# The opening of a two-layer block: row tiles loaded in six pieces, the filters' first layer in another PSUM bank, the second conditioning chunk straight behind the first

## The chip, the cores and the metric

The kernel runs on one core of a Trainium2 chip. A core has TensorE (PE; its weight loads are listed apart as PEld), VectorE (DVE), ScalarE (ACT), GpSimd (POOL) and SyncE (SP), which here issues all transfers of the opening. Results of TensorE go to PSUM. The metric is the device time of one execution in microseconds (us), as the median of several runs.

## The reference

Two layers act on a sequence `x` of 512 rows and a context `ctx` of 256 rows, each row 1024 wide. Every layer has conditioned norms, a mixer and a convolutional feed-forward part. Layer 0 mixes with Fourier transforms and a long convolution (hyena), layer 1 with attention. What the opening computes is this:

```python
sh1, sc1, g1, sh2, sc2, g2 = _adaln(c, w_mod[0], b_mod[0])    # silu(c) @ w_mod + b_mod, in six parts
hx = _modulate(_rms_norm(x, norm1[0]), sh1, sc1)              # rms_norm * (1 + sc1) + sh1
csh1, csc1, ... = _adaln(c_ctx[None, :], w_mod[0], b_mod[0])
hc = _modulate(_rms_norm(ctx, norm1[0]), csh1, csc1)
proj = h @ w_in                                               # first projection of the mixer, h = hx or hc
...
h = jnp.sin(f * (z @ _f32(w1) + _f32(b1)))                    # hyena filters, layer by layer
h = jnp.sin(f * (h @ _f32(w2) + _f32(b2)))
h = jnp.sin(f * (h @ _f32(w3) + _f32(b3)))
```

## The kernel before

Rows lie along the free axis and the 1024 features along partitions. So `x` is eight row tiles of 128 partitions (`KD` = 8), each 772 columns wide: 512 columns of `x`, two of zeros, 256 columns of `ctx` from column `C0` = 514 on, and two of zeros. Matmuls are split in three (`mm3`): a high part of weight and operand, made on ACT (`hi`, L133), and a low part, made on VectorE (`lo`, L138).

The opening is in `mixer`, under a manual schedule: PE, VectorE, ACT and SyncE execute in the order in which the code is written. In that order:

- SyncE loads the filters' tables (`zT`, `fw`), then `x` in eight transfers of 256 KB (L460) and `ctx` in eight of 128 KB (L462). Behind them come two conditioning chunks `wm` of 2 MB in two halves each (`gemv_raw`, L209) and three tiles of the projection's weight (`wraw`, L146). The pool of chunks has two buffers, so the third chunk's load waits for the first chunk's matmuls.
- PE computes the filters' first layer (`layer(0, None, 0)`, L410), then `spare(8)`. `spare(n)` is n matmuls of the identity with a constant tile into a PSUM bank that is overwritten later; their result is not used. In the profile each counts as two passes of L470.
- The norms: `s1(d)` and `s2(d)` square row tile d on ACT (L267), for `x` and then for `ctx`, and add it up on VectorE (L274). `f1(True, 0)` and `f2(True, 0)` fold the sums over partitions on PE (L280) and take the reciprocal root on VectorE (L167 to L176). `f1(True, 1)` and `f2(True, 1)` spread the root over partitions on PE (L298) and copy it out of PSUM on ACT (L301).
- Conditioning: `gemv_pe` multiplies a chunk on PE (L219) and copies the result on ACT (L222). The function that it returns (`g0`, `g1`: the turn) turns it into columns on PE (L227) and adds the bias on VectorE (L232). Scale and shift of the norm's first four row tiles need chunks 0 and 1.
- `layer(0, pa, 1)` is the sine's argument on VectorE (L384 to L393), step 2 the sine itself on ACT (L414).
- `both(d, 0)` makes the normalised high part of row tile d (L308 on VectorE, L309 on ACT), `both(d, 1)` the low part (L313), and `first(m, k)` is the projection of row tile k onto output tile m (L158 to L160).

PSUM is given out in two kinds: `mm`, three tiles of two banks, all three held by the projection (`ps3`), and `ms`, two tiles of one bank. Norm folds, spreads, gemvs, turns and the filters' layers take turns with the two `ms` tiles.

Of the kernel before, what the change touches and what calls it, by code (L numbers as in the profile page):

```python
# [9 lines left out]
F32 = mybir.dt.float32  # L10
# [8 lines left out]
P = 128  # L19
D = 1024  # L20
KD = 8
T = 512
C = 256
C0 = 514
TW = 772
# [60 lines left out]
class Builder:  # L86
# [309 lines left out]
    def filter_mlp(self):  # L396

        nc, I = self.nc, self.I
        p = self.pf
        zT = self.t(p, [66, 384], F32, "zT")  # L400
        fw = self.t(p, [P, 3, P], F32, "fw")
        self.w4 = self.t(p, [P, 1024], F32, "w4")
        nc.sync.dma_start(zT, I["zT"])
        nc.sync.dma_start(fw, I["fw"])

        def layer(l, h, step):
            if step == 0:
                ps = self.ms()
                K = 66 if l == 0 else P
                nc.tensor.matmul(ps[:, :384], fw[:K, l, :], (zT if l == 0 else h)[:K, :384], start=True, stop=True)  # L410
                return ps
            if step == 1:
                return self.sine(h, self.col(f"fb{l + 1}"))
            nc.scalar.activation(h[:, :384], h[:, :384], AF.Sin)  # L414
            return h

        return layer
# [15 lines left out]
    def mixer(self):  # L433
        nc, I = self.nc, self.I
        v = nc.vector
        self.S2 = self.pool("S2", bufs=19)
        xp = self.pool("xp", side="right")
# [7 lines left out]
            v.memset(self.onesN[nh], nh)  # L445
        self.altr = self.t(self.pf, [P, 1], F32R, "altr")
        v.tensor_copy(self.altr, self.alt)
        x = [self.t(xp, [P, TW], F32, f"x{d}") for d in range(KD)]
        hh, hl = [], []
        (s1, f1, a1), (s2, f2, a2) = self.norm(0, 0, x, hh, hl, 0, T, tp), self.norm(0, 0, x, hh, hl, C0, C, tp)  # L450
        self.bscale = 1.0
# [3 lines left out]
        with self.tc.manual_schedule(engines={ENG.PE, ENG.DVE, ENG.SP, ENG.Activation}):  # L455
            layer = self.filter_mlp()
            warm = tp()[:, 0:256]
            v.memset(warm, 1.0)
            for d in range(KD):
                nc.sync.dma_start(x[d][:, 0:512], I["xT"][d])  # L460
            for d in range(KD):
                nc.sync.dma_start(x[d][:, C0 : C0 + C], I["cxT"][d])  # L462
            wm = [self.gemv_raw(0), self.gemv_raw(1)]
            win = [self.wraw(I["w_in"][m]) for m in range(3)]
            ps3 = [self.mm() for _ in range(3)]

            def spare(n):

                for _ in range(n):
                    nc.tensor.matmul(ps3[2][:, 512:768], self.ident, warm, start=True, stop=True)  # L470

            pa = layer(0, None, 0)
            spare(8)
            for d in range(KD):
                s1(d)
            for d in range(KD):
                s2(d)
            f1(True, 0)
            spare(5)
            f2(True, 0)  # L480
            spare(3)
            f1(True, 1)
            g0 = self.gemv_pe(0, 0, wm[0])
            wm.append(self.gemv_raw(2))
            f2(True, 1)
            h = layer(0, layer(0, pa, 1), 2)
            g0()
            spare(3)
            wins = [self.wsplit(win[0])]
            g1 = self.gemv_pe(0, 1, wm[1])  # L490
            spare(1)
            wm.append(self.gemv_raw(3))
            nc.sync.dma_start(self.w4, I["w4"])
            for tt in (4, 5):
                dec[tt] = tp()
                nc.sync.dma_start(dec[tt], I["decay"][tt])
            wins.append(self.wsplit(win[1]))
            g1()
            self.make_A(0, 0, b=4)
            for d in range(KD):  # L500
                hh.append(self.t(hp, [P, TW], F32R, f"hh{d}"))
                hl.append(self.t(hp, [P, TW], F32R, f"hl{d}"))
            self.zero_pads(hh + hl)

            def both(d, step):
                a1(d, step)
                return a2(d, step)

            def first(m, k):
                self.proj_k(ps3[m], wins[m], hh, hl, k)

            pa = layer(1, h, 0)
            spare(5)
            both(0, 0)
            both(1, 0)
            both(0, 1)
            first(0, 0)
            first(1, 0)  # L520
            wins.append(self.wsplit(win[2]))
            both(1, 1)
            both(2, 0)
            first(0, 1)
            first(1, 1)
            both(3, 0)
            both(2, 1)
            first(2, 0)
            first(2, 1)
            g2 = self.gemv_pe(0, 2, wm[2])  # L530
            both(3, 1)
            h = layer(1, layer(1, pa, 1), 2)
            first(0, 2)
            g2()
            first(1, 2)
            first(2, 2)
            g3 = self.gemv_pe(0, 3, wm[3])
            first(0, 3)
            g3()
            self.make_A(0, 0, a=4)  # L540
            first(1, 3)
            first(2, 3)
            self.close("wm")
            self.pg = self.pool("pg")
            for d in range(4, KD + 1):
                if d < KD:
                    last_act = both(d, 0)
                if d > 4:
                    last = both(d - 1, 1)
                    for m in range(3):  # L550
                        first(m, d - 1)
                if d == 6:
                    pa = layer(2, h, 0)
                if d == 4:
                    self.filter_w4()
            h3 = layer(2, layer(2, pa, 1), 2)
            nc.sync.dma_start(self.brow, I["hyb"].partition_broadcast(P))
            for j in range(2):
                nc.sync.dma_start(self.sb[:, j, :], I["cboth"][j : j + 1, :].partition_broadcast(P))
# [1386 lines left out]
```

## Time and profile before

| | |
|---|---|
| median of 3 runs | 1623.88 us (1619.55 to 1624.58) |
| the profiled execution | 1623.17 us |
| its span, first to last instruction | 1621.4 us |
| mean granted TensorE clock | 0.993 |
| loads, mean over the span | 107 GB/s |
| loads, first 45 us | 356 GB/s |

The span is what the profile shows; the execution's own time has 1.8 us more around it. "Busy" is the union of an engine's instructions; DMA issues and waits on SyncE are not counted as busy. A row of the timeline gives start, length, engine, line, operation, output<-input and count, and in brackets the idle time of the engine before it with what ended it. The chain of waits follows back from the last instruction to whatever released each step. "DMA to landing" runs from the issue of a transfer to the arrival of its last byte's signal.

### The profile page before, as it was taken

To read this page: it belongs to the slowest core of one execution; us is meant where nothing else is said; L and a number is where in the kernel's file an instruction comes from. 1 tells how busy PE (TensorE), PEld (TensorE's weight loads), DVE (VectorE), ACT (ScalarE), POOL (GpSimd) and SP (SyncE) were. 2 spreads that over 40 slices of the span, in tenths; PEclk is the share of its full clock that TensorE was granted. 3 is DMA by queue.
4 is the path that set the end of the run, shared out by engine and by line. 5 is a ranking of instruction groups with operands and counts; after the bars stand their busy time and mean duration, and the time that the engine had idled before them with its cause. 6 is when DMAs were issued, how large, how long until landed. Compare 5 with 4: busy or idle time off the path is not lost.

```text
span 1621.4 us, 20798 instructions
## 1 busy us (share of the span) xinstructions
PE 1585.4 (98%) x8248; PEld 1295.8 (80%) x8248; DVE 1047.0 (65%) x1702; ACT 620.5 (38%) x883; POOL 108.7 (7%) x165
## 2 busy tenths in 40 slices
PE   7999998999999999999999999999999999999999
PEld 5787888888888888888888887666559878878887
DVE  6789869878786354643354586899987544344243
ACT  4441234434222212322123246998954433233131
POOL 0022134000000000000000001122210000000000
PEclk9999998999999999999999999999999999999999
DMA  9336412533443143431343210000034233233222
GB/s 355 107 116 214 163 36 76 191 118 108 166 156 130 65 143 130 156 131 65 111 140 110 91 57 20 13 11 14 0 105 142 79 104 104 78 104 104 78 91 91
DMA packets 54541, 173.35 MB, mean 107 GB/s; under 512 B 6187, under 2 KB 9453, under 8 KB 53421
## 3 DMA queue, kind: packets, MB, share of 16 engines
q1 hardware_dynamic: 54445, 172.03, 30.8%
q8 instruction: 65, 1.06, 0.3%
q14 instruction: 31, 0.25, 0.0%
HBM read 166.24 MB, written 5.77 MB: 106 GB/s over the span
## 4 chain that ended last, share of the span: by engine, by line
PE 82%; DVE 13%; ACT 2%; issue 2%; POOL 1%; DMA 1%; SPq 0%; POOLq 0%; ACTq 0%; DVEq 0%
PE mm L158 24%; PE mm L160 24%; PE mm L159 24%; PE pv L1614 2%; DVE S L1590 2%; DVE junk L243 1%; DVE wl L138 1%; PE s L1560 1%; DVE wr L1629 1%; ACT wh L133 1%; PE mm L616 1%; DVE mx L1574 0%; PE k L159 0%; PE ms L219 0%; PE k L160 0%
## 5 line engine op out<-in xcount | busy, mean ns | idle before, releaser
L158 PE MATMUL mm<-hh,wh 128*128 128x512 f32 (+2 forms) x1360 | 479.8, 355 | 1.8 <-ACT wh L133 0.9
L159 PE MATMUL mm<-hl,wh 128*128 128x512 f32 (+2 forms) x1360 | 477.9, 352 | 2.3 <-DVE hl L313 2.3
L160 PE MATMUL mm<-hh,wl 128*128 128x512 f32 (+2 forms) x1360 | 477.2, 351 | 1.6 <-DVE wl L138 1.6
L133 ACT ACTIVATE wh<-wr 128x1024 fp32r<-128x1024 f32 (+1 forms) x192 | 197.8, 1033 | 571.8 <-PE mm L159 530.4
L138 DVE TENSOR_TENSOR wl<-wr,wh 128x1024 fp32r<-128x1024 f32 (+2 forms) x192 | 230.9, 1205 | 235.8 <-ACT wh L133 229.2
L158 PEld LDWEIGHTS mm<-hh,wh 128*128 128x128 f32 x1360 | 256.2, 189 | 49.0 <-issue 7.6
L159 PEld LDWEIGHTS mm<-hl,wh 128*128 128x128 f32 x1360 | 256.4, 189 | 39.2 <-DVE hl L313 3.5
L160 PEld LDWEIGHTS mm<-hh,wl 128*128 128x128 f32 x1360 | 256.2, 188 | 37.5 <-DVE wl L138 2.2
L243 DVE SCALAR_TENSOR_TENSOR junk<-wr,sb 128x1024 bf16<-128x1024 f32 x128 | 156.1, 1219 | 41.2 <-DMA wr<-wmodT 41.1
L160 PE MATMUL mm<-ah,wl 128*128 128x512 f32 (+1 forms) x480 | 172.2, 359 | 0.0
L158 PE MATMUL mm<-ah,wh 128*128 128x512 f32 (+1 forms) x480 | 172.0, 359 | 0.0
L159 PE MATMUL mm<-al,wh 128*128 128x512 f32 (+1 forms) x480 | 171.7, 358 | 0.0
L1143 DVE SCALAR_TENSOR_TENSOR xr<-mm,mod,xr 128x512 f32<-128x512 f32 (+1 forms) x100 | 61.6, 630 | 153.8 <-PE mm L160 153.6
L159 PEld LDWEIGHTS mm<-al,wh 128*128 128x128 f32 x480 | 90.4, 188 | 14.4 <-DVE al L138 0.2
L158 PEld LDWEIGHTS mm<-ah,wh 128*128 128x128 f32 x480 | 90.3, 188 | 14.2 <-issue 0.3
L160 PEld LDWEIGHTS mm<-ah,wl 128*128 128x128 f32 x480 | 90.3, 188 | 14.1
L1614 PE MATMUL pv<-S,V 128*128 128x512 f32 x192 | 93.8, 597 | 2.5 <-ACT S L1593 2.5
L1175 ACT ACTIVATE fg<-fg 128x772 f32<-128x772 f32 (+1 forms) x44 | 32.6, 741 | 97.8 <-DVE fg L375 91.1
L1568 ACT ACTIVATE S<-s,rks 128x512 f32<-128x512 f32 x96 | 62.7, 686 | 12.4 <-PE pv L1614 8.5
L1614 PEld LDWEIGHTS pv<-S,V 128*128 128x128 f32 x192 | 34.4, 190 | 34.8 <-issue 29.4
L1590 DVE TENSOR_TENSOR S<-S,mx 128x1536 f32<-128x1536 f32 x32 | 55.3, 1749 | 2.3 <-POOL mx L1586 2.3
L1586 POOL PARTITION_ALL_REDUCE mx<-mx x16 | 44.9, 2806 | 163.2 <-DVE mx L1583 163.2
(337 smaller groups left out, 2263.1 us busy)
## 6 DMA issues: line engine op xcount, KB each, us to landing
wr<-w_up SPq DMA_DIRECT2D x88, 512.0 KB, 3.2
wr<-wmodT SPq DMA_DIRECT2D x80, 512.0 KB, 3.2
wr<-w_dn SPq DMA_DIRECT2D x32, 512.0 KB, 3.3
wm<-wmod0a SPq DMA_DIRECT2D x8, 1024.0 KB, 10.3
wr<-w_in SPq DMA_DIRECT2D x16, 512.0 KB, 4.2
wr<-w_out SPq DMA_DIRECT2D x13, 512.0 KB, 3.5
wr<-w_dn SPq DMA_DIRECT2D x17, 384.0 KB, 3.1
wr<-w_o SPq DMA_DIRECT2D x11, 512.0 KB, 3.3
```

The lines of the kernel that those rows point to most:

```text
L133: self.nc.scalar.activation(dst, src, AF.Copy)
L138: (eng or self.nc.vector).tensor_tensor(dst, src, hi.bitcast(F32), op=ALU.subtract)
L158: mmul(out, wh, xh, start=start, stop=False)
L159: mmul(out, wh, xl, start=False, stop=False)
L160: mmul(out, wl, xh, start=False, stop=stop)
L243: nc.vector.scalar_tensor_tensor(junk, raw, 1.0, self.sb[:, j, :], op0=ALU.mult, op1=ALU.mult, accum_out=acc)
L1143: nc.vector.scalar_tensor_tensor(x[m][:, a2:b2], ps[:, a2:b2], mod[:, 8 * sec + m, c : c + 1], x[m][:, a2:b2], op0=ALU.mult, op1=ALU.add)
L1175: nc.scalar.activation(g[:, :n], g[:, :n], AF.Silu)
L1568: nc.scalar.activation(c.S[a][j // 3][:, j % 3, :], c.ps[a, j], AF.Copy, scale=c.r[:, g : g + 1])
L1586: nc.gpsimd.partition_all_reduce(c.m[a][:, 1, :], c.m[a][:, 0, :], P, bass.bass_isa.ReduceOp.max)
L1590: v.tensor_tensor(c.S[a][h], c.S[a][h], mb.to_broadcast([P, 3, T]), op=ALU.subtract)
L1614: nc.tensor.matmul(c.P[a], V[:, j, o : o + 128], c.S[a][j // 3][:, j % 3, :], start=j == 0, stop=j == 5)
```

## The change

All row tiles become one tile `xx` of 128 x 8 x 772; `x[d]` is a view of it, and everything behind the opening uses these views as it used the tiles. `x` is loaded in four transfers of two row tiles, `ctx` in two transfers of four, each 512 KB. The filters' first layer writes to `ps3[1]` instead of an `ms` tile. Of the spare matmuls, five become four, three become one, and another three go. The second chunk's `gemv_pe` and the load of the fourth chunk come directly behind the first chunk's turn, ahead of the split of the first weight tile.

```diff
-        def layer(l, h, step):
+        def layer(l, h, step, ps=None):
             if step == 0:
-                ps = self.ms()
+                ps = self.ms() if ps is None else ps
...
-        x = [self.t(xp, [P, TW], F32, f"x{d}") for d in range(KD)]
+        xx = self.t(xp, [P, KD, TW], F32, "x")
+        x = [xx[:, d, :] for d in range(KD)]
...
-            for d in range(KD):
-                nc.sync.dma_start(x[d][:, 0:512], I["xT"][d])
-            for d in range(KD):
-                nc.sync.dma_start(x[d][:, C0 : C0 + C], I["cxT"][d])
+            for d in range(0, KD, 2):
+                nc.sync.dma_start(xx[:, d : d + 2, 0:512], I["xT"][d : d + 2].rearrange("d p n -> p d n"))
+            for d in range(0, KD, 4):
+                nc.sync.dma_start(xx[:, d : d + 4, C0 : C0 + C], I["cxT"][d : d + 4].rearrange("d p n -> p d n"))
...
-            pa = layer(0, None, 0)
+            pa = layer(0, None, 0, ps3[1])
             spare(8)
...
             f1(True, 0)
-            spare(5)
+            spare(4)
             f2(True, 0)
-            spare(3)
+            spare(1)
             f1(True, 1)
             g0 = self.gemv_pe(0, 0, wm[0])
             wm.append(self.gemv_raw(2))
             f2(True, 1)
             h = layer(0, layer(0, pa, 1), 2)
             g0()
-            spare(3)
+            g1 = self.gemv_pe(0, 1, wm[1])
+            wm.append(self.gemv_raw(3))
             wins = [self.wsplit(win[0])]
-            g1 = self.gemv_pe(0, 1, wm[1])
             spare(1)
-            wm.append(self.gemv_raw(3))
             nc.sync.dma_start(self.w4, I["w4"])
```

## The prediction

> **What bounds the kernel now.** I read the page first, then the chain of waits from 0 to 60 us, then the timeline of the same stretch, last the DMA view and the table by stretches. From the page:
>
> ```profile
> span 1621.4 us, 20798 instructions
> PE 1585.4 (98%) x8248; PEld 1295.8 (80%) x8248; DVE 1047.0 (65%) x1702; ACT 620.5 (38%) x883; POOL 108.7 (7%) x165
> ```
>
> TensorE is busy 98% of the span, so a change to other engines pays only where TensorE has nothing useful to do. One such place is the opening, up to the first projection matmul. The chain there (start, length, what):
>
> ```profile
> 6.28 5.77 DMA x<-xT
> ...
> 19.42 1.40 PE mm L470 x6
> 20.82 0.91 PE ms L298 x8
> 21.75 0.59 ACT s L301
> 22.39 1.97 PE ms L219 x16
> 24.38 0.60 ACT s L222
> 25.02 0.72 PE ms L298 x4
> 25.77 0.38 ACT s L301
> 26.19 1.05 PE ms L227 x8
> 27.25 1.40 PE mm L470 x6
> 28.65 1.90 PE ms L219 x16
> 30.62 0.59 ACT s L222
> 31.21 0.97 ACT wh L133
> 32.20 1.23 DVE wl L138
> ```
>
> L470 is the spare matmul, whose result nobody reads (two passes each, so x6 is spare(3)); it stands in the chain twice for 1.40 us. L219 is a conditioning chunk (gemv), L227 its turn, L298 the spread of a norm's factor, L133 and L138 the split of a weight. The timeline adds what the chain hides:
>
> ```profile
> 2.96 3.75 SPq L460 DMA_DIRECT2D x<-xT  x8
> 6.44 1.26 ACT L267 ACTIVATE s<-x 128x512 f32<-128x512 f32 x2 [1.04 <-DMA x<-xT]
> 6.76 5.64 SPq L462 DMA_DIRECT2D x<-cxT  x8
> 8.69 6.67 ACT L267 ACTIVATE s<-x 128x512 f32<-128x512 f32 x14 [0.99 <-DMA x<-xT]
> 9.35 8.18 DVE L274 TENSOR_TENSOR s<-s,s 128x512 f32<-128x512 f32 x13 [0.93 <-ACT s L267]
> 12.45 2.11 SPq L209 DMA_DIRECT2D wm<-wmod0a  x4
> ...
> 19.62 0.16 DVE L176 SCALAR_TENSOR_TENSOR rq_r<-rq_b,rq_r 128x4 f32<-128x4 f32 x1
> ...
> 21.75 0.16 DVE L176 SCALAR_TENSOR_TENSOR rq_r<-rq_b,rq_r 128x2 f32<-128x2 f32 x1 [0.52 <-PE ms L298]
> ...
> 22.42 0.67 DVE L384 TENSOR_SCALAR s<-ms,pcol 128x384 f32<-128x384 f32 x1
> ...
> 25.70 0.36 DVE L393 TENSOR_SCALAR s<-s 128x384 f32<-128x384 f32 x1
> ...
> 28.36 1.06 ACT L133 ACTIVATE wh<-wr 128x1024 fp32r<-128x1024 f32 x1 [1.68 <-DMA wr<-w_in]
> ...
> 32.91 2.32 PE L470 MATMUL mm<-s,cst 128*128 128x256 f32 x10
> 35.29 0.51 PE L158 MATMUL mm<-hh,wh 128*128 128x512 f32 x1
> ```
>
> Three things are to be seen. The sums of squares on VectorE end at 17.53 and its reciprocal root at 19.78, yet the spread starts only behind the spare matmuls. The gemv at 22.39 waits for the copy that empties a small PSUM bank: the filters' first layer has held one of the two since 5.7 us, until L384 reads it at 22.42. And the loads are a limit of their own:
>
> ```profile
> SPq L462 <- DMA x<-xT: 2.2, 6, 0.6
> ```
>
> This row of SyncE's waits says that six context transfers were held back until an earlier transfer landed. The transfers behind them, the second half of gemv chunk 1 and the second w_in, by their issue and by the time from issue to landing:
>
> ```profile
> 13.86 0.70 SPq L209 DMA_DIRECT2D wm<-wmod0a  x1
> wm<-wmod0a SPq DMA_DIRECT2D x1, 1024.0 KB, 13.2
> wr<-w_in SPq DMA_DIRECT2D x1, 512.0 KB, 13.3
> ```
>
> The half lands at 27.1. The w_in row is of the issue that follows the first w_in's, at about 16.3, and lands at 29.6; the first has landed by 28.36 by ACT's wait above. Behind 35 us TensorE hardly waits at all; its largest wait from 35 to 200 us, in total, times and longest, is
>
> ```profile
> PE mm L159 <- DVE hl L313: 2.3, 3, 0.9
> ```
>
> It waits there for VectorE's low parts, and these move along with the first projection. So what the opening gains or loses should reach the end whole.
>
> **The change, part by part.**
>
> *Loads in pieces.* Sixteen issues become six. The bytes and the runs in memory (2 KB and 1 KB) stay. A piece of two row tiles is usable only when its second half is there. From the squares' rows, tiles 2 to 7 come between 8.69 and 12.05 (the chain's last x landing), so 0.67 us apiece. The square of tile 0 therefore starts some 0.6 later than 6.44, and that of tile 2 at about 9.35 instead of 8.69. VectorE's adds run back to back from 9.35 to 17.53, so the whole row moves by about 0.65: sums end at 18.15, the first reciprocal root at 20.4. Bounds: nothing later, if fewer and larger transfers run 10% faster, and 1.3 later, if the pieces land one tile apart more. I take 0.65. [...]
>
> SyncE gets free early: four pieces and two context pieces at about 0.47 each end near 5.8 instead of 12.4, and the eight-in-flight limit then lets the wm and w_in issues follow landings, from about 6 on. What that is worth:
>
> ```profile
> 9.00:11.00 2.00, 2.00 (x7) 1.56 (x6) 1.44 (x3) 1.90 (x4) 0.00 (x0) 1.00 1.02 388
> 13.00:15.00 2.00, 0.92 (x9) 0.92 (x9) 1.69 (x5) 2.00 (x8) 0.00 (x0) 1.00 0.90 283
> 15.00:17.00 2.00, 2.00 (x7) 1.64 (x7) 1.69 (x4) 0.35 (x2) 0.00 (x0) 0.51 0.96 377
> 17.00:19.00 2.00, 2.00 (x9) 1.63 (x7) 1.65 (x10) 0.00 (x0) 0.00 (x0) 0.64 1.00 406
> 23.00:25.00 2.00, 1.31 (x16) 0.13 (x4) 1.86 (x5) 0.59 (x1) 0.00 (x0) 1.00 0.99 416
> 50.00:60.00 10.00, 9.14 (x59) 6.64 (x59) 6.02 (x14) 4.37 (x8) 0.00 (x0) 1.00 0.09 30
> ```
>
> (columns: busy time of PE, PEld, DVE, ACT, POOL; granted clock, DMA share, GB/s.) At 13 to 15 us the loads run at 283 GB/s instead of 388: 105 GB/s for 2 us is 0.21 MB, or 0.5 us at 388. That dip is the queue running dry before wm, and I count it as removed. The gemv half then lands at 26.6, the two w_in at 27.8 and 29.1. Bounds: nothing gained, and 1.5 us, if late single engines of the queue catch up too.
>
> *First layer in another bank.* No instruction is added. The bank is one that the projections first write after 33 us, and the sine reads it by 23. Both small banks are then free, so the gemv no longer waits for the copy L301 (0.59), nor the second spread for the copy L222.
>
> *Fewer spares.* The spread now follows one spare, not three. It starts with its factor at 20.4, 0.25 earlier than now despite the later sums, and ends at 21.45. Gemv 0 follows at once: 21.5 to 23.4. VectorE's second root loses its 0.52 wait but starts 0.62 later, so ends about 22.6; the second spread runs to 24.1, the copies on ACT to 24.5 (0.60 and 0.38), the turn of chunk 0 to 25.2. It now ends at 27.25: two microseconds are gone. The sine keeps its length (22.42 to 26.06 now) and starts 0.1 later.
>
> *Second chunk behind the first turn.* spare(3) (1.40) is gone from ahead of it, and the split of the first w_in stands behind its copy on ACT. What is late next is the load: the gemv could start at 25.2, but its second half of 0.95 waits for 26.6 and ends at 27.6. The reissue of the buffer, gemv_raw(3), stands behind it in SyncE's queue with w4 and the decays, all earlier by the same. On ACT: copy to 28.25, then both splits, 1.06 each, to 30.4 (both w_in are there). Today the first split lies in ACT's idle time before the copy; now it is on the path, and this gives back 1.06 of the gain. VectorE's split of the second w_in takes 1.23, to 31.65. Today it ends at 33.43 and the first projection starts 1.86 behind it; with that the first projection starts at 33.5.
>
> *Sum.* 35.29 less 33.5 is 1.8 us gained. With the load no earlier it is 1.3 (everything behind the gemv half moves by 0.5); with the load 1.5 earlier the gemv runs 25.2 to 27.1, and it is 2.3. The profiled execution took 1623.17 us, its span 1621.4 and 1.8 around it, 0.7 under the median of the runs, 1623.88. Less 1.8 that gives 1621.4. About 0.3% (4.9 us) is what a measurement of this kernel can tell from no change: the three runs alone lie 5.0 apart.
>
> **The rivals.**
>
> *The gain is swallowed behind 35 us.* Loads for the filter stage come off the same queue, and if they land no earlier, TensorE waits where it did not. Time: 1623.2. Against it: from 50 to 60 us the queue moves 30 GB/s, so the opening's loads are done by then. For it: VectorE and GpSimd work behind 42 us in an order of their own.
>
> *The granted clock drops once or twice more.* After 13 to 15 us, with TensorE busy 0.92 of 2 us, the clock was 0.51 and then 0.64: (1 − 0.51) × 2 + (1 − 0.64) × 2 = 1.7 us of TensorE's time lost. Six spares fewer leave it emptier between 23 and 33. One such drop there, where gemv, turn, layer and spare(5) stand one behind the other ahead of the first projection, takes the gain: 1623.1. Two in a row make it 1624.8, slower than before. It decides when a stretch falls to about 0.92 in 2 us. By my sum, 25.2 to 33.5 holds 1.90 (gemv) + 1.05 (turn) + 2.32 (spares) + about 1.2 (layer and one spare, at the spares' rate by columns) = 6.5 of 8.3 us, or 1.6 in 2, above the 1.31 of 23 to 25 where the clock stayed at 1.00. So it is unlikely. [...]
>
> *The pieces are waited for across columns.* In one tile the context columns of four row tiles stretch, first to last, over the others' x columns. If waits go by that extent, the squares of tiles 1 to 3 wait for a context piece, at 13.5 by the landing pace, and the sums end near 23.3, 5.1 later than in my sum; 0.4 of this is slack at the gemv's load, and the first projection comes at about 38.1: 1626.0. Against it: today's square at 6.44 did not wait for context columns of the same tile, issued from 6.76 on; but those two ranges do not interleave.
>
> *The change does not do what it says* only where the pieces would land as singles do; that is the lower bound of the 0.65.
>
> **How the numbers follow.** Forecast 0.60 (1620.9 to 1621.9 by the bounds of the load); swallowed 0.16; clock 0.08; columns 0.06; something that none of these rows shows, 0.05 to either side. The likeliest gives 1621.4. The range takes in the cases up to the clock's, and on both sides half of the 5.0 us over which the runs spread: 1618.5 to 1625.5. Faster by over 4.9 us needs more than any row here offers: 0.07. Slower by over 4.9 needs the worst case and more: 0.07. Within: 0.86.
>
> **What would show it.** Right: six issues that end by about 6 us and wm issues from then on; sums that end near 18.1; gemv 0 starting straight behind the first spread near 21.5 with no wait for L301; gemv 1 stalled in its middle by its load until about 26.6; the first projection at 33 to 34; granted clock 1.00 from 20 us on. Wrong: squares that wait past 13 us (columns), a granted clock under 1 between 24 and 35 (gate), or a new TensorE wait between 35 and 100 us (swallowed). A time outside the range with a first projection near 33.5 would say that the opening does not reach the end.

## The result, and the profile after

| | before | changed |
|---|---|---|
| median | 1621.74 us (1619.17 to 1624.58, 18 runs) | 1624.84 us (1620.99 to 1628.63, 18 runs) |
| ratio | | 1.0023, 95% interval 1.0016 to 1.0029 |
| the profiled execution | 1623.17 us | 1626.17 us |
| its mean granted clock | 0.993 | 0.990 |

The change makes the kernel slower, by some 0.2%. The page of the changed kernel shows nearly the same work (twelve TensorE passes fewer, those of the six spares) in a longer span:

```profile
span 1624.4 us, 20766 instructions
PE 1585.1 (98%) x8236; PEld 1296.0 (80%) x8236; DVE 1047.6 (64%) x1702; ACT 620.1 (38%) x883; POOL 108.6 (7%) x165
```

**The opening came out as forecast.** The timeline of the changed kernel from 2 to 36 us (start, length, engine, line; in brackets the idle time and what ended it):

```profile
2.97 2.35 SPq L461 DMA_DIRECT2D x<-xT  x4
5.37 1.91 SPq L463 DMA_DIRECT2D x<-cxT  x2
7.32 3.29 SPq L209 DMA_DIRECT2D wm<-wmod0a  x4
8.12 1.15 ACT L267 ACTIVATE s<-x 128x512 f32<-128x512 f32 x2 [2.51 <-DMA x<-xT]
10.36 8.18 DVE L274 TENSOR_TENSOR s<-s,s 128x512 f32<-128x512 f32 x13 [0.36 <-ACT s L267]
...
20.94 1.13 PE L298 MATMUL ms<-cst,rq_r 128*128 128x128 f32 x8 [0.41 <-DVE nrm_s L285]
22.00 1.92 PE L219 MATMUL ms<-wm,sT 128*32 128x512 f32 x16
23.85 0.71 PE L298 MATMUL ms<-cst,rq_r 128*128 128x128 f32 x4
24.63 1.05 PE L227 MATMUL ms<-cst,s 128*128 128x2 f32 x8
25.61 1.92 PE L219 MATMUL ms<-wm,sT 128*32 128x512 f32 x16
28.14 2.01 ACT L133 ACTIVATE wh<-wr 128x1024 fp32r<-128x1024 f32 x2
33.47 0.50 PE L158 MATMUL mm<-hh,wh 128*128 128x512 f32 x1 [1.21 <-ACT hh L309]
```

The first square starts at 8.12 instead of 6.44 and the adds end at 18.54 instead of 17.53. The gemv (22.00) stands straight behind the spread, with no wait for the copy L301, and the second chunk behind the first turn. The first projection comes at 33.47 instead of 35.29. From 40 to 159 us each instruction of VectorE stands 1.8 us ahead of its counterpart in the kernel before: up to there the gain arrives whole.

**The loss lies 940 us later.** TensorE's waits from 960 to 990 us have one row in the changed kernel, and none in the kernel before:

```profile
PE k L158 <- DVE kp L1437: 2.4, 1, 2.4
```

The timeline of the changed kernel there, and then that of the kernel before:

```profile
971.31 1.50 PE L1332 MATMUL ms<-cst,rq_r 128*128 128x128 f32 x12
974.13 1.00 DVE L1437 SCALAR_TENSOR_TENSOR kp<-mm,pcol,ropeK 64x772 f32<-64x772 f32 x1
975.19 0.53 PE L158 MATMUL k<-wh,qah 128*128 128x192 f32 x1 [2.38 <-DVE kp L1437]
```

```profile
974.01 1.50 PE L1332 MATMUL ms<-cst,rq_r 128*128 128x128 f32 x12
975.27 0.34 PE L158 MATMUL k<-wh,qah 128*128 128x192 f32 x1
976.84 1.00 DVE L1437 SCALAR_TENSOR_TENSOR kp<-mm,pcol,ropeK 64x772 f32<-64x772 f32 x1
```

L1332 spreads the factor of attention's compressed keys; the row `k<-wh,qah` is the first query projection of attention, into a PSUM tile named `k2` (K2 below). L1437 makes the rotary keys `kp` out of another PSUM tile, the rotary projection. Before, the query started 1.26 us behind L1332 and `kp` was made later, at 976.84; now the query waits for `kp` and starts 3.88 behind L1332, 2.6 more. At L1332 the changed kernel is 2.70 us ahead of the old one, at the query 0.08. (Of the 2.70 the opening gave 1.8; the rest came near 189 us, where only the old kernel's execution ran at half clock, from 189.10 for 3.41 us.)

The clock follows in this execution. Table by stretches of the changed kernel, then of the kernel before (busy time of PE, PEld, DVE, ACT, POOL; granted clock, DMA share, GB/s):

```profile
972.00:974.00 2.00, 0.81 (x8) 0.62 (x6) 0.93 (x2) 1.55 (x4) 2.00 (x6) 1.00 0.46 167
974.00:976.00 2.00, 0.81 (x4) 0.81 (x5) 2.00 (x4) 0.83 (x3) 0.42 (x1) 0.79 0.00 0
976.00:980.00 4.00, 4.00 (x21) 4.00 (x20) 0.07 (x1) 0.00 (x0) 0.00 (x0) 0.50 0.00 0
980.00:984.00 4.00, 4.00 (x16) 3.51 (x16) 2.26 (x5) 0.81 (x1) 0.00 (x0) 0.50 0.00 0
984.00:988.00 4.00, 4.00 (x10) 2.31 (x9) 1.18 (x3) 1.84 (x4) 0.41 (x1) 0.50 0.01 4
```

```profile
976.00:980.00 4.00, 4.00 (x33) 3.70 (x32) 3.59 (x6) 2.34 (x5) 1.12 (x3) 1.00 0.01 5
980.00:984.00 4.00, 4.00 (x13) 2.88 (x12) 2.57 (x7) 2.32 (x5) 0.68 (x1) 0.62 0.01 4
984.00:988.00 4.00, 3.84 (x15) 2.34 (x14) 2.77 (x4) 0.92 (x2) 0.14 (x1) 0.95 0.00 0
```

By the trace's record of the clock, the changed kernel runs at half clock from 975.16 for 13.65 us, the old one from 981.0 for 3.41 us. The difference of 10.24 us at a granted clock of 0.50 is 5.1 us of TensorE's time, by my estimate. Together: 2.7 us ahead at L1332, 4.7 behind at 1000, 3.0 behind at the end of the span. The 1.7 us between come back from 1200 to 1530 us, where neither trace shows half clock; why was not followed up.

**Why the query waits.** The three `mm` slots of PSUM are handed out in the order of first use, and from then on in turn. Before, the spare matmuls touched `ps3[2]` first; now the filters' first layer touches `ps3[1]` first. In the compiled program's placement, `ps3` moves from banks (4, 2, 0) to banks (2, 0, 4), and every later `mm` tile of this pool is shifted likewise. 940 us later attention closes this pool and opens another, whose first tile, K2, takes banks 0 and 1. The rotary projection lay in bank 2 before and lies in bank 0 now, so the first query may only be written when `kp` has read it.

### The profile page after: what moved, and what is told of

Its sections match the earlier page's. It is cut to its first block, busy times and chain, and to the rows that moved or that the text cites. A ratio compares the mean times of both kernels' runs of the same rounds, so it can differ in the third digit from the quotient of the medians.

```text
span 1624.4 us, 20766 instructions
## 1 busy us (share of the span) xinstructions
PE 1585.1 (98%) x8236; PEld 1296.0 (80%) x8236; DVE 1047.6 (64%) x1702; ACT 620.1 (38%) x883; POOL 108.6 (7%) x165
## 3 DMA queue, kind: packets, MB, share of 16 engines
q8 instruction: 65, 1.06, 0.3%
## 4 chain that ended last, share of the span: by engine, by line
PE 80%; DVE 14%; issue 2%; ACT 2%; DMA 1%; POOL 1%; POOLq 0%; SPq 0%; DVEq 0%; ACTq 0%
PE mm L158 24%; PE mm L159 23%; PE mm L160 23%; PE pv L1614 2%; DVE S L1590 2%; DVE wl L138 2%; PE s L1560 1%; DVE wr L1629 1%; DVE junk L243 1%; DMA wr<-wmodT 1%; DVE hl L313 1%; ACT wh L133 1%; PE k L159 1%; PE k L158 1%; PE mm L616 1%
```

## The experiments

Two theories stood at first. **Slots**: the layer's move to `ps3[1]` reorders the PSUM slots, and that wait with its clock is the loss. **Clock**: the tile does not matter; the earlier opening only shifts the program in time, and the half-clock stretch behind 972 us falls as that shift happens to set it. All that the runs show of windows of the clock are such stretches: at 0.50, 3.41 us or a multiple of it long, with starts that lie multiples of 3.413 us apart (last section); what sets them no run shows. The changed kernel compares with 18 runs of the kernel before, the others with 29 to 33 on the same chip, the last two with 21. They ran on several chips, on which the kernel before had medians of 1620.73 to 1622.61, so the ratios are to be compared and not the medians.

| kernel | median us | ratio to before (95%) | mean clock, before's | first projection |
|---|---|---|---|---|
| changed | 1624.84 | 1.0023 (1.0016 to 1.0029) | 0.9919 | 33.47 |
| layer in the spares' bank | 1623.21 | 1.0002 (0.9993 to 1.0011) | 0.9925, 0.9935 | 33.57 |
| slots alone | 1625.34 | 1.0021 (1.0009 to 1.0033) | 0.9939, 0.9935 | 36.41 |
| layer in small bank | 1625.44 | 1.0019 (1.0009 to 1.0029) | 0.9909, 0.9935 | 38.99 |
| K2 elsewhere | 1621.46 | 0.9997 (0.9987 to 1.0006) | 0.9925, 0.9935 | 33.46 |
| single loads | 1621.22 | 0.9997 (0.9988 to 1.0007) | 0.9930, 0.9939 | 34.09 |
| spares back | 1620.17 | 0.9990 (0.9981 to 0.9999) | 0.9939, 0.9939 | 33.23 |
| order undone | 1620.32 | 0.9991 (0.9982 to 0.9999) | 0.9936, 0.9939 | 33.00 |
| wait filled | 1625.59 | 1.0022 (1.0012 to 1.0033) | 0.9924, 0.9939 | 34.45 |
| pieces and bank | 1620.02 | 0.9989 (0.9981 to 0.9998) | 0.9937, 0.9942 | 35.80 |
| bank alone | 1619.69 | 0.9986 (0.9977 to 0.9994) | 0.9945, 0.9942 | 32.20 |
| pieces alone | 1622.95 | 1.0007 (0.9998 to 1.0016) | 0.9942, 0.9942 | 35.65 |
| K2 elsewhere, spares back | 1621.68 | 0.9998 (0.9990 to 1.0007) | 0.9935, 0.9942 | 33.60 |
| no spares | 1622.80 | 1.0011 (1.0001 to 1.0021) | 0.9908, 0.9947 | 36.30 |
| bank, more spares | 1619.84 | 0.9991 (0.9982 to 1.0000) | 0.9945, 0.9947 | 34.05 |

**The layer in the bank of the spares.** This keeps the old order of first use and everything else of the change.

```diff
-            pa = layer(0, None, 0, ps3[1])
+            pa = layer(0, None, 0, ps3[2])
```

> The kernel after, with the filters' first layer in ps3[2] (the tile of the spare matmuls) instead of ps3[1]; all else as after. Theory S (slots): the first tile of ps3 that is touched takes the lowest PSUM slot, and the order of the three slots is handed on to attention; with ps3[1] first, the tile K2 of the first query matmuls comes to lie over the tile that the key norm still reads, and those matmuls wait 2.4 us at about 973 us and then run at half clock. With ps3[2] first, as in the kernel before, K2 lies over another tile: no wait of PE k L158, first projection at 33.5 as after, 1619 to 1620.5 us. Theory C (clock phase): the earlier opening only moves the program against the clock gate's windows; the tile does not matter: 1624 to 1625, the stretch at half clock near 975 us stays.

The opening is the changed kernel's (first projection 33.57), and no wait stands before the first query. Table by stretches of this kernel:

```profile
972.00:974.00 2.00, 2.00 (x21) 2.00 (x19) 0.34 (x2) 0.96 (x3) 1.83 (x4) 1.00 0.76 249
974.00:976.00 2.00, 2.00 (x20) 1.90 (x18) 2.00 (x4) 1.42 (x3) 1.01 (x3) 1.00 0.01 3
976.00:980.00 4.00, 4.00 (x19) 2.74 (x19) 3.46 (x8) 1.79 (x3) 0.00 (x0) 0.80 0.02 4
```

TensorE is busy through 972 to 976. The profiled execution took 1619.78 us, the fastest of its eleven, but the median, 1623.21, is only level with the kernel before, and above the 1619 to 1620.5 of its theory. So the slots explain the loss against before, not where the 1.7 us of the opening went.

**The slots alone.** The kernel before with the spare matmuls in `ps3[1]`.

```diff
-                    nc.tensor.matmul(ps3[2][:, 512:768], self.ident, warm, start=True, stop=True)
+                    nc.tensor.matmul(ps3[1][:, 512:768], self.ident, warm, start=True, stop=True)
```

> The kernel before, with the spare matmuls in ps3[1] instead of ps3[2], nothing else. Theory S: the opening keeps its time (first projection at 35.3), but the slot order of after comes with it: a wait of PE k L158 for the key norm of about 2.4 us near 976 us, part of the time at half clock behind it, 1624.5 to 1627. Theory C: as before, 1621 to 1622.5, no new wait.

The opening takes as long as before (14.63 us from spread to first projection in both). The wait is there, as TensorE's only one from 960 to 990 us in this kernel:

```profile
PE k L158 <- DVE kp L1437: 2.4, 1, 2.4
```

One changed index in a matmul that nobody reads costs 1.0021, as much as the whole change. The query starts 3.87 us behind L1332, as in the changed kernel. But the clock behind the wait stays at 1.00 here, in this kernel's table by stretches:

```profile
976.00:980.00 4.00, 1.62 (x15) 1.43 (x14) 2.87 (x5) 2.37 (x5) 2.47 (x6) 1.00 0.26 89
980.00:984.00 4.00, 4.00 (x33) 3.70 (x32) 0.95 (x2) 0.81 (x1) 0.00 (x0) 1.00 0.02 4
```

Half clock comes only at 985.49, for 3.41 us, as long as in the kernel before, and over all runs the mean clock is not below that of before (0.9939 and 0.9935). So the wait alone already costs its 2.6 us (`kp` 1.35 us behind before's, the query 3.97), and the long stretch at half clock is a second loss that comes in some executions only. Two of the eleven runs, 1631.68 and 1631.84 us at a clock of 0.991, stand 3.6 us above the next; that they are the ones with the long stretch is not shown.

**The first query's tile elsewhere.** The changed kernel, with K2 taken behind the rotary tiles, so that it lies over a bank that was read long before.

```diff
-            q0 = K2()
             rt, prot = MS(), [S1(), S1()]
+            q0 = K2()
```

> The kernel after, with the order turned in which attention takes its PSUM tiles: the one small tile and two score tiles first, K2 behind them, so that K2 lies over the query projection's tile, which has long been read. The opening is untouched. Theory S: the wait of PE k L158 goes, and with it the half clock behind it: 1619 to 1621. Theory C: as after, 1624 to 1625.

No wait before the query, the changed opening (33.46), ratio 0.9997, the median just above the 1619 to 1621 expected. The wait goes without touching the opening, so it hangs on the overlap of the two tiles and not on the layer's bank as such. The profiled execution, at 1625.84 us the slowest of the eleven, still ran at half clock for 6.83 us from 979.08 and again from 1248.73: clock can be lost there without the wait.

**The layer back in the small bank.** The changed kernel with `pa = layer(0, None, 0)`.

> The kernel after, with the filters' first layer back in a small bank (ms); pieces, spares and second chunk as after. Theory S: no wait of PE k L158; the gemv of chunk 0 waits again for the copy of the first spread, so the first projection comes 0 to 1 us later than after (33.5 to 34.5): 1619.5 to 1621. Theory C: 1624 to 1625.

The wait before the query is gone, but the granted clock fell to half three times up to 44 us, in this kernel's table by stretches:

```profile
18.00:20.00 2.00, 2.00 (x8) 1.36 (x6) 1.69 (x11) 0.00 (x0) 0.00 (x0) 0.50 1.04 434
20.00:24.00 4.00, 3.15 (x14) 1.98 (x16) 2.81 (x16) 0.59 (x1) 0.00 (x0) 0.50 1.00 417
24.00:28.00 4.00, 3.29 (x18) 0.63 (x11) 2.87 (x7) 0.59 (x1) 0.00 (x0) 0.62 0.93 377
28.00:32.00 4.00, 3.54 (x26) 1.76 (x27) 0.17 (x1) 0.80 (x2) 0.00 (x0) 0.81 0.96 349
32.00:36.00 4.00, 4.00 (x23) 2.37 (x16) 1.24 (x2) 2.49 (x3) 0.00 (x0) 0.76 0.92 320
36.00:40.00 4.00, 2.33 (x10) 1.45 (x8) 3.96 (x9) 1.78 (x4) 0.00 (x0) 1.00 0.99 413
40.00:44.00 4.00, 3.65 (x12) 2.99 (x12) 3.32 (x4) 1.34 (x2) 1.74 (x2) 0.59 0.95 327
```

The first projection came at 38.99 where 33.5 to 34.5 was expected: with few spares and the waits for the small banks back, TensorE stands idle more often (busy for 3.15, 3.29 and 3.54 of 4 us from 20 to 32 us, against 3.59, 3.94 and 3.87 with the layer in the spares' bank), and clock is lost in the opening itself. The median, 1625.44, is above both theories' ranges. This profile, at 1629.42, is the slowest of the ten runs; six of them had a clock of 0.992 or more where this one had 0.988.

**The wait filled.** The changed kernel with ten identity matmuls ahead of the first query, into a part of a tile that nobody reads.

```diff
+            for _ in range(10):
+                nc.tensor.matmul(prot[1][:, 384:512], self.ident, self.ident, start=True, stop=True)
             QT(pairs[0], 0)
```

> The changed kernel as it is, with its wait before the first query matmul, and with ten identity matmuls ahead of that matmul, into a bank that nobody reads (the free end of the second score tile), about 2.4 us in all by the twelve passes in 1.50 us of L1332. Theory that the half-clock stretch from 975 to 989 us follows from TensorE's idle 2.4 us: the wait itself stays (the query matmul starts at 975.2), the granted clock stays at 1.00 behind it up to the stretch at about 981 that the kernel before has too, the attention gains 2 to 5 us in the profile, and the median is 1622.0 to 1623.5 against 1624.84 of the changed kernel. Rival, that the half clock there comes from the short matmuls behind 980.5 and not from the wait: same clock rows, median as the changed kernel's, 1624.5 to 1625.5.

The timeline of this kernel:

```profile
973.22 1.50 PE L1332 MATMUL ms<-cst,rq_r 128*128 128x128 f32 x12
976.18 2.50 PE L1692 MATMUL s<-cst 128*128 128x128 f32 x20 [1.46 <-DVE pt L1339]
978.43 0.33 PE L158 MATMUL k<-wh,qah 128*128 128x192 f32 x1
```

The filling missed its place: its own bank came free only behind another VectorE read, so it waited 1.46 us and then stood in the query's way, which starts 5.21 behind L1332. The median is no better, 1625.59, as the rival said, but not for the rival's reason. The clock stays at 1.00 until 983.7 and falls for one stretch of 3.41 us instead of 13.65. One execution does not show that the filling did this, since "slots alone" has the whole wait and the same 3.41. But none of the seven runs has a clock under 0.991, and half of the changed kernel's 18 have: it fits that the long stretch goes with the idle time.

**The parts of the opening.** Six kernels take the change apart, all with the old order of slots. The edits of the first three, against the changed kernel with the layer in `ps3[2]`:

```diff
 # single loads: separate row tiles and sixteen transfers, as before
+            for d in range(KD):
+                nc.sync.dma_start(x[d][:, 0:512], I["xT"][d])
+            for d in range(KD):
+                nc.sync.dma_start(x[d][:, C0 : C0 + C], I["cxT"][d])
 # spares back
-            spare(4)
+            spare(5)
             f2(True, 0)
-            spare(1)
+            spare(3)
 # order undone: the old order behind g0()
+            spare(3)
+            wins = [self.wsplit(win[0])]
             g1 = self.gemv_pe(0, 1, wm[1])
+            spare(1)
             wm.append(self.gemv_raw(3))
-            wins = [self.wsplit(win[0])]
-            spare(1)
```

> The changed kernel with the filters' first layer in ps3[2] (so that the slots stand as before) and with x loaded as before: separate row tiles, sixteen transfers. Everything else of the change stays. Theory that the pieces bring the loads forward: without them the issues on SyncE end near 12 us again instead of 6, the second half of gemv chunk 1 and the w_in tiles land about 1 us later, and the first projection comes at 34.3 to 34.8 us instead of 33.57 in the run with the bank of the spares; median 0.7 to 1.2 us above that run. Rival, that the order of the second chunk and the free small bank bring all of the gain: the sums end 0.6 earlier (near 17.6), the first projection comes at 33.0 to 33.6, and the median is the same as in that run or up to 0.5 lower.

> The changed kernel with the first layer in ps3[2] and with the spare matmuls of the norms back, five and three. Theory that the missing spares cost granted clock: in the runs so far the mean granted clock of the changed openings was 0.9925 against 0.9935 of the kernel before, which is 1.6 us of 1622. With the spares back the mean clock is 0.9935 again, the first projection comes at 33.6 to 34.6 (one spare is 0.47 us, of which part lies in waits), and the median is 0.5 to 1.5 us lower than that of the run with the bank of the spares alone. Rival, that the spares only stand in the way: the clock stays at 0.9925 and the median is 0 to 1 us higher.

> The changed kernel with the first layer in ps3[2] and with the old order behind the first turn: spare(3), the split of the first w_in, then the second chunk. Theory that the order is worth its 1.40 us of spares less the split that moves onto the path: first projection at 34.3 to 35.0, 0.7 to 1.4 later than with the new order, and the median higher by as much. Rival, that the free small bank and the early loads bring all of the gain and the order none: first projection at 33.4 to 33.8 and no difference in the median.

"Spares back" has the clock of the kernel before (0.9939 both), as its theory said, and a first projection (33.23) earlier than expected.

"Pieces and bank" undoes both the order and the spares; "bank alone" is the kernel before with nothing but the layer in `ps3[2]`; "pieces alone" is the kernel before with nothing but the six pieces.

> The kernel before with the six pieces and with the first layer in ps3[2], the bank of the spares; all spare matmuls and the order of the second chunk as before. Theory that these two parts carry the whole gain, and that fewer spares and the new order only give some back: first projection at 33.0 to 33.8 us (the run with the order undone had 33.00), mean granted clock 0.9935 or more, median 1.0 to 2.0 us below the kernel before, ratio 0.9988 to 0.9994. Rival, that the new order is needed: first projection at 34.3 or later, ratio 0.9995 to 1.0005.

> The kernel before with the first layer in ps3[2] and nothing else. Theory that the bank is the larger part: gemv 0 no longer waits for the copy of the spread, the second chunk is then held by its load near 27, first projection at 34.2 to 34.8, median 0.5 to 1.1 us below the kernel before. Rival, that the bank alone gives nothing since the load ends last anyway: first projection at 35.0 to 35.4, same median.

> The kernel before with the six pieces and nothing else (first layer in the small bank as before, all spares, old order). Theory that the pieces alone are worth little, since gemv 0 still waits for the copy of the spread and the second spread for the copy of gemv 0: the sums end 0.5 to 1.0 later, the loads 1 earlier, first projection at 34.9 to 35.6, median within 0.5 us of the kernel before. Rival, that the loads were the limit: first projection at 34.0 to 34.5, median about 1 lower.

A single profile's first projection moves with the clock, so I split it in two: the end of the sums, and the time from the first spread to the first projection.

| kernel | sums end | spread to first projection |
|---|---|---|
| before | 17.53 | 14.63 |
| pieces alone | 17.91 | 14.63 |
| bank alone | 17.01 | 12.79 |
| pieces and bank | 18.30 | 12.72 |
| order undone (pieces, bank, fewer spares) | 17.81 | 12.79 |
| spares back (pieces, bank, order) | 18.32 | 12.52 |
| changed | 18.54 | 12.53 |
| single loads (bank, order, fewer spares) | 17.84 | 13.85 |

The bank is worth 1.84 us and nearly all of the gain. The new order adds 0.27 with the early loads. Without them it loses 1.06, since the second chunk then stops for its load, in the waits of "single loads":

```profile
PE ms L219 <- DMA wm<-wmod0a: 1.1, 1, 1.1
```

The pieces bring the loads forward, but by themselves gain nothing. The sums end at 17.8 to 18.5 with them and at 17.0 to 17.8 with single loads in this table, but at 18.66 in "slots alone", which has single loads too. Over all sixteen profiles the mean is 18.29 with the pieces (eleven profiles) and 17.70 without (five): 0.6 apart, as I had forecast, but the five alone spread over 1.65, so no single profile shows it. "Order undone" came at 33.00, earlier than either of its expectations, and without a loss, as its rival had said; "single loads" fell between its two expectations (34.09), its ratio (0.9997, against 1.0002 with the pieces) nearer to the rival's. "Bank alone" came at 32.20, earlier than either expectation, and gained more than either: it was not held by its load, and its opening kept the clock, as its timeline and then its table by stretches show:

```profile
20.47 1.92 PE L219 MATMUL ms<-wm,sT 128*32 128x512 f32 x16
...
25.48 1.92 PE L219 MATMUL ms<-wm,sT 128*32 128x512 f32 x16
...
32.20 0.50 PE L158 MATMUL mm<-hh,wh 128*128 128x512 f32 x1
```

```profile
14.00:16.00 2.00, 2.00 (x13) 1.84 (x13) 1.64 (x4) 1.01 (x3) 0.00 (x0) 1.00 0.92 359
16.00:18.00 2.00, 1.81 (x11) 1.33 (x10) 1.67 (x8) 0.00 (x0) 0.00 (x0) 1.00 1.03 434
```

"Pieces and bank" came at 35.80 in its profile, late as its rival had said, but not for want of the new order: its opening ran at half clock from 15.37 for 6.83 us, and from the spread on it is as short as "order undone" (12.72). Over all runs it is 0.9989, as the theory said. Bank alone has the lowest ratio, 0.9986 (0.9977 to 0.9994). It is one of four kernels whose interval lies below 1, with "spares back", "order undone" and "pieces and bank"; these runs do not tell the four apart.

**Both losses mended.** K2 elsewhere and the spares back, on the changed kernel:

> The changed kernel with its own bank for the first layer, with the query tile taken behind the rotary tiles (so that it lies over a bank read early) and with the spare matmuls of the norms back, five and three. Theory that the two mended losses add up: no wait before the first query matmul, first projection at 33.2 to 34.0, mean granted clock 0.9935 or more, median 1.5 to 2.5 us below the kernel before and about 4 below the changed kernel. Rival, that the spares did nothing and the run with them back was only a lower draw: ratio to before 0.9997 as without them.

First projection 33.60, no wait, but 0.9998: the two mends did not add up. Against "spares back" (0.9990) it differs by less than the two intervals' widths.

**Do missing spares cost clock?** A large dose: the changed kernel with the layer in `ps3[2]` and no spare behind the first eight.

```diff
-            spare(4)
+            spare(0)
             f2(True, 0)
-            spare(1)
+            spare(0)
 ...
-            spare(1)
+            spare(0)
 ...
-            spare(5)
+            spare(0)
```

> The changed kernel with the first layer in ps3[2] and with no spare matmul behind the first eight: the one behind the first fold, the one behind the second, the one behind the second chunk and the five ahead of the first projection are all gone. Theory that a changed opening with few spares loses granted clock, which is what the run with the bank of the spares (mean clock 0.9925 against 0.9935 of the kernel before, ratio 1.0002) then paid with most of its 1.7 us: with none at all the opening has two or more half-clock windows up to 45 us, the mean clock is 0.991 or less, and the ratio 1.0005 to 1.002. Rival, that the spares do not matter there and that run was a high draw: one half-clock window up to 45 us, mean clock as in the kernel before, ratio 0.9985 to 0.9995.

Its table by stretches:

```profile
16.00:18.00 2.00, 0.66 (x5) 0.57 (x4) 1.58 (x5) 1.09 (x4) 0.00 (x0) 0.55 1.00 418
20.00:24.00 4.00, 2.70 (x12) 1.98 (x16) 2.69 (x18) 0.59 (x1) 0.00 (x0) 0.50 1.00 414
32.00:36.00 4.00, 0.94 (x4) 0.32 (x3) 3.90 (x8) 1.46 (x3) 0.00 (x0) 0.66 1.00 414
36.00:40.00 4.00, 3.13 (x8) 2.34 (x9) 3.32 (x6) 2.65 (x5) 0.00 (x0) 0.50 0.99 409
```

Two stretches of 10.24 us at half clock, mean clock 0.9908, ratio 1.0011: they do. "Spares back" differs from this kernel only in fourteen spares, and its interval (0.9981 to 0.9999) lies below this one's (1.0001 to 1.0021). Together the spares pay for themselves, though nobody reads what they compute. The other side of the test, the bank alone with `spare(12)` for `spare(8)`:

> The kernel before with the first layer in ps3[2], and with twelve spare matmuls ahead of the first fold instead of eight (the four more are some 1.9 us, about what TensorE waits there for the sums). Theory that this wait is where the opening's half-clock window comes from: no window at half clock up to 45 us, first projection at 32 to 33.5, mean granted clock 0.995 or more, ratio 0.997 to 0.9985. Rival, that the windows behind 130 us take the same time whatever the opening does: ratio as with the bank alone, 0.9985 to 0.999.

The record of the clock has no half clock up to 45 us, but the ratio is 0.9991, with a clock of 0.9945 as with the bank alone and a first projection at 34.05 instead of 32 to 33.5: the rival. The stretches at 131 and 244 us came all the same.

## Why the prediction was wrong

- **The opening: right in its end, in part by luck.** Sum 33.5, measured 33.47; the experiments put the same 1.8 us on one edit, the bank. Inside the sum two terms were off and cancelled. The first piece landed at 8.10 and not about 7.0 (first square 1.7 late instead of 0.6; sums 18.54 instead of 18.15); in the eleven profiles with pieces the first square starts anywhere from 7.09 to 8.38. The six issues ended at 7.28 and not near 5.8. (The limit of eight transfers in flight is in both traces: before, the six context issues that waited start at 8.68, 9.33, 10.01, 10.68, 11.36 and 12.07, each as the x piece of eight issues earlier lands, the last of them 5.8 us behind its issue at 6.28; changed, the first w_in issue starts at 11.06, as the third piece lands, 7.1 behind its issue at 3.96.) And the second chunk was not held by its load: its second half had landed by 25.33, where I had it at 26.6, so it started late, at 25.61 instead of 25.2, and yet ended at 27.53 as I had it at 27.6.
- **"No instruction is added. The bank is one that the projections first write after 33 us": the step that failed.** I costed the move by who reads and writes that bank in the opening. It also changes which slot is touched first, and so the bank of every `mm` tile that follows in this pool. I put that at nothing; it comes back at 973 us as a wait of 2.4 us. Slots alone, 1.0021; slots mended, from 1.0023 to 1.0002.
- **"What the opening gains or loses should reach the end whole": wrong.** The row of waits that carried it looked at 35 to 200 us only. Nothing there changed; what did was beyond it, and in no trace of before, since before had no wait there. My "something that none of these rows shows" had 0.05 on the slow side. The median of 1624.84 lies inside my range of 1618.5 to 1625.5 only because the range is wide: it moved the other way.
- **The clock rival ("gate"): clock was lost, but in another place.** I looked for lost clock between 23 and 33 us, and there it was 1.00. It was lost behind the wait, where I had none. Its bound of about 0.92 us busy in 2 was an estimate from one row of before; the last section has 4.00 us busy in 4 with half clock 1 us behind them. That the median meets my price for two drops, 1624.8, is luck: none of the 18 runs lies between 1623.6 and 1626.1. They fall into two groups: nine at a clock of 0.988 to 0.990 and 1626.1 to 1628.6 us, nine at 0.992 to 0.996 and 1621.0 to 1623.6. The second is about what 1621.7 − 1.8 + 2.6 = 1622.5 gives, the forecast plus the wait; the first is the same with the 5.1 us of the long half-clock stretch, 1627.6. That the groups are this stretch is inferred from the sizes: of the changed kernel only an execution of the first group was profiled.
- **Pieces waited for across columns, gain swallowed before 100 us:** neither happened; the squares begin at 8.12, and the 1.8 us still stand at 159.

What stays open: with the slots mended, the changed kernel gains none of its 1.7 us (1.0002 and 0.9997), while the same with its spares or its old order does (0.9990, 0.9991). The mean clock of the first two is 0.0010 under that of before, 1.6 us, and no spares at all make that 0.0039. This points to the six missing spares, of which "spares back" and "order undone" each put three back, but "K2 elsewhere, spares back" at 0.9998 does not fit, and the intervals are too wide to decide. An estimate from the runs helps: time fitted to granted clock over each kernel's runs and its runs of before (about 1 us for 0.001) puts "K2 elsewhere" 1.6 us and "no spares" 1.7 us below the kernel before at equal clock, the bank of the spares 0.7, each with a standard error of some 0.4. By this estimate at least part of the gain is there, and lost clock takes it.

## What to carry to other kernels

A tile that is first used earlier changes more than its own place: where buffers are handed out in turn, it shifts all that follow, and the price can lie in a stage that the edit never mentions. So list the placements before and after, and look for tiles of the next stage that now lie over one still being read. And take a change apart: here moving one tile out of a small bank was worth nearly the whole gain, the choice of the bank gave back more than that, and the pieces and the order added next to nothing.

## What the runs showed of the hardware

In the two traces the stretches at half clock start on a grid. In the kernel before they start at 15.03, 134.49, 189.1, 247.13 and 981.0 us: 0, 35, 51, 68 and 283 times 3.413 us apart from the first; in the changed kernel at 16.02, 132.07, 244.71 and 975.16: 0, 34, 67 and 281 times. (One more at the very end of each span is left out, and the record of the clock begins only at 11.61 and 12.61 us.) Their lengths, here and in the experiments, are multiples too (3.41, 6.83, 10.24, 13.65). The 3.413 us is read off these starts and lengths.

The grid stands differently against the same wait in two executions, and clock was lost behind it in one of them. In the changed kernel the whole wait of 2.38 us falls between two points of the grid, 971.75 (one step before 975.16) and 975.16; TensorE is busy for 1.06 of these 3.41 us, and the clock halves at 975.16. In "slots alone" a point of the grid, 978.66 (two steps before the half clock at 985.49), cuts the same wait in two; TensorE is busy for 1.61 us of the 3.41 before it and for 2.84 behind it, and the clock stays at 1.00 there. With one execution of each, that this is the reason is not shown.

In the kernel before the clock halves behind a stretch in which the profile shows TensorE busy throughout: it is busy for 4.00 of 4.00 us from 976 to 980, and at 981.0 the clock halves. In that stretch stand the short matmuls of one column (L1444, `32x1`, from 978.1), and half clock follows within 3.2 us of their start in all thirteen profiles without the wait, for 3.41 us in eleven and 6.83 in two. That these matmuls are the reason was not tested.
